# A hybrid attention backbone: the last head and the output tiles of layer 1 become pieces of the listed order

## Chip, cores and metric

The kernel runs on one core of a Trainium2 chip. A core has five engines that run side by side, each through its own queue in order: PE (matrix products), DVE (vectors), ACT (activations), POOL (general vectors) and SP (which here only issues DMAs). The metric is the device time of one execution in microseconds (us); the result is the median over several runs.

## What is computed

Two layers over 1024 latent tokens of width 1024 with 256 context tokens. Layer 0 is multi-head latent attention, layer 1 differential attention, which the change touches:

```python
def combine(o1, o2, gate):
    o = o1 - lam_full.astype(o1.dtype) * o2
    o = rms_norm(o, g_sub) * (1.0 - lambda_init)
    return gated(o, gate)
...
o1, o1_c = prefix_attention(q[:, :, :, 0:1], k[:, :, :, 0], v, ...)
o2, o2_c = prefix_attention(q[:, :, :, 1:2], k[:, :, :, 1], v, ...)
...
x = layer_norm(DEEPNORM_ALPHA * x + gate[:, None, :] * (o @ out_w[i]), ln_g[i], ln_b[i])
```

Eight heads each have two softmaxes over 1280 keys; the second, times lambda, is taken from the first; the result times the values is normed per head and gated with SiLU; then come the output projection, the residual and a layer norm. Only the 1024 latent rows of layer 1 are wanted.

## The kernel before

Everything is float32 in effect: an operand is split into a high and a low part, and a product is three matmuls (`mm3`, L202 to L206), high by high, high by low, low by high.

Layer 1 works in tiles of 128 query rows, 8 tiles (t = 0 to 7) for each of 8 heads (h = 0 to 7). Attention of one tile (`attend`, L1896 on) has these steps, with the names used below: **scores** (five chunks on PE), **maxima** and a bound (DVE), **exponentials** (ACT), sums and the **join** of the two softmaxes (DVE), the **far half** (a split on ACT and DVE and a transposing DMA on SP, tiles `dd` to `pd`), **turns** of the near half (transposes on PE into the PSUM bank `ps_t`, high part `ph` on ACT, low part `pl` on DVE), **values** (30 matmuls on PE into `ps_t`), the output with a square for the norm (ACT), the norm (POOL), and a store of the tile's result to DRAM (`o_d`, SP).

Beside the attention of head h run the projections of head h + 1: keys, queries and values (`ps_s` on PE), with splits, rotary terms and gates on the other engines. Their gate goes through SiLU into `gg` and then to DRAM as `sg_d`.

The order of this work is not written out by hand. `heads1` (from L1664) describes every step as a piece with an engine, a cost, its inputs and outputs, and a due time; `Plan.run` (L1596 on) simulates the five engines and lists the pieces in the order in which it starts them. The due time is the place in the loop plus an offset per kind (table `OFF`, L46); `EPS1` and `AHEAD` say how far a piece may be taken ahead. All five engines then run in exactly that order (`MAN2`). Tiles have rings of buffers: one bank `ps_t`, four `ps_p` and one `ps_c` for scores, two `ps_s`.

Before, that list holds heads 0 to 6 and the projections of head 7. After it stands another stage, written by hand (`step1`, L2083, and the loops behind it), in which only PE's order is fixed and the eight banks go round as one ring `ps_b`:

- `out_open` (L1451) opens buffers in the place of the projections' inputs, and splits four of the eight output weights; their raw form, `z` and `res`, was loaded and multiplied by the layer's gate (`x.gate`, L1891) at the end of the list.
- attention of head 7 (`scores1`, `turn1`, `turn_far`, `values1`, L1356 to L1432), tile by tile.
- beside it, two tiles behind, the output: `out_load` (L1470) fetches the seven finished heads `o_d` and the gates `sg_d` and multiplies them on POOL; `out_turn` (L1480) transposes the tile on PE and splits it into `wx` and `wy`; `out_tile1` (L1501) does 16 groups of three products, adds the residual and takes the layer norm on DVE, ACT and POOL.

Of the kernel before, what the change touches and what calls it, by code (L numbers as in the profile page):

```python
# [9 lines left out]
F32 = mybir.dt.float32  # L10
# [7 lines left out]
P = 128  # L18
# [25 lines left out]
EPS1 = dict(P=0.05, A=0.05, D=0.2, G=0)  # L44
AHEAD = 3.0
SP0, SP1, SP2 = 0.0, 0.3, 3.3  # L46
OFF = {"bound0": -4.5, "bound1": -0.65, "exp0": -0.45, "exp1": -0.65, "far.hi": -4.3, "far.lo": -2.35, "far.move":
       0.25, "g.add": 0.55, "g.bias": -0.5, "g.keep": 0.45, "g.load": 0.4, "g.sum": -0.9, "g.zero": -1.35, "join":
       -0.6, "k.ctx": -5.4, "k.hi": -0.4, "k.lo": -3.7, "k.move": 2.65, "max.c": -0.05, "max0": -5.7, "max1": 0.2,
       "o.hi": 2.55, "o.lo": 0.15, "o.load": -1.65, "o.mul": -1.85, "open": 2.2, "prod": 0.3, "pv": -5.35,  # L50
       "pv.norm": -0.8, "pv.out": -0.05, "pv.sq": -3.0, "pv.store": -2.0, "pv.us": 0.35, "q.hi": -0.6, "q.lo": -0.1,
       "q.move": 1.95, "r.add": 0.45, "r.cos": 1.1, "r.out": 1.4, "r.sin": -1.3, "r.swap": -0.15, "score0": 0.45,
       "score1": 0.4, "scorec": 0.05, "sums": -3.55, "turn.hi0": -1.25, "turn.hi4": -1.2, "turn.lo0": 0.9,
       "turn.lo4": -3.25, "turn0": -0.6, "turn4": 0.5, "v.gate": 1.3, "v.hi": 1.3, "v.keep": 0.7, "v.lo": 1.65,
       "v.octx": -0.25, "v.out": 2.05, "v.pctx": 0.05, "v.silu": 1.2, "v.store": 6.05, "v.turn": -2.25, "w.hi": 1.2,
       "w.lo": 0.4, "w.load": -0.6, "w.root": -1.2, "w.scale": 0.55, "w.sq": 0.95, "w.sum": -6.25, "w.unit": 0.95,
       "w.us": -1.3, "x.gate": 1.15, "x.load": 5.2, "x.mul": 4.6}
# [5 lines left out]
SLOTO = 0, 7000, 7000, 7000, 7000  # L63
# [9 lines left out]
def hybrid_kernel(  # L73
# [1282 lines left out]
    def scores1(h, t):  # L1356

        ks = kt1[h]
        q1, qs = qt1[h]
        ts = slice(t * P, (t + 1) * P)  # L1360
        mx, sm = w1("mx"), w1("sm")
        p = [w1("p0"), w1("p1")]

        def st_of(out, m, c0, n):
            pe.matmul(out, qs[m][:, ts], ks[m][:, c0:c0 + n], start=True, stop=False)
            pe.matmul(out, q1[m][:, ts], ks[m][:, c0:c0 + n], start=False, stop=True)

        st = {}

        def chunk(c0, ms):  # L1370
# [78 lines left out]
    def out_open():  # L1449
# [10 lines left out]
        for k, w in enumerate(pre):  # L1460
# [5 lines left out]
            if k == 0:  # L1466
                out_load(1)
# [737 lines left out]
```

## Time and profile before

| | before |
|---|---|
| median of 3 runs | 1737.77 us (1737.37 to 1739.45) |
| the profiled execution | 1738.9 us, span 1737.1 us |
| PE busy | 1632.8 us (94%) |
| DVE busy | 1252.4 us (72%) |
| ACT busy | 1150.4 us (66%) |
| POOL busy | 903.6 us (52%) |

The span is from the first to the last record of the trace; the execution's own time has a little around it. The listed stage of layer 1 runs from about 950 to 1565 us of the span, the stage written by hand from there to the end. Busy time is what an engine's instructions took; matmuls are pipelined, so their durations overlap and a busy PE need not be at its peak. The granted clock is the share of full speed that PE had. A wait is given with the engine and tile that ended it, the sum, the number and the longest.

### The profile page before, as it was taken

How to read it: one execution, taken by the hardware profiler on the slowest of the kernel's cores; microseconds unless marked ns; L12 is line 12 of the kernel's file. 1: busy time of each engine (PE TensorE's matmuls, PEld its weight loads, DVE VectorE, ACT ScalarE, POOL GpSimd, SP SyncE). 2: the span in 40 equal slices, each digit the busy share in tenths (PEclk: the TensorE clock that was granted, in tenths of full speed). 3: DMA queues.
4: the chain of work that ended last, by engine and by line, in shares of the span. 5: the costliest groups of instructions: out<-in, count | busy, mean ns of one | idle time of the engine just before them, and what ended most of it. 6: DMA issues, size and time to landing. Idle time of an engine off the chain costs nothing.

```text
span 1737.1 us, 36492 instructions
## 1 busy us (share of the span) xinstructions
PE 1632.8 (94%) x14308; PEld 1203.3 (69%) x14308; DVE 1252.4 (72%) x2005; ACT 1150.4 (66%) x2228; POOL 903.6 (52%) x772
## 2 busy tenths in 40 slices
PE   7999999999999999899999999999999999995997
PEld 6989966566656656567776676767676767583776
DVE  7658765566565575746763889898989898976664
ACT  2552167777867867855563887878787878776452
POOL 1522047666867867764645526262626363636454
PEclk9999999999999999999999999999999999997999
DMA  8258530111111121335532344434333344334442
GB/s 311 85 148 245 163 96 23 37 35 39 37 35 39 37 60 26 110 138 185 162 130 69 77 103 96 102 97 103 93 76 96 79 92 107 62 96 137 122 126 79
DMA packets 183930, 171.63 MB, mean 99 GB/s; under 512 B 82023, under 2 KB 159431, under 8 KB 183758
## 3 DMA queue, kind: packets, MB, share of 16 engines
q1 hardware_dynamic: 175358, 161.69, 34.0%
q10 hardware_dynamic: 8400, 7.61, 1.3%
q8 instruction: 112, 1.84, 0.5%
q14 instruction: 60, 0.49, 0.1%
HBM read 98.65 MB, written 27.07 MB: 72 GB/s over the span
## 4 chain that ended last, share of the span: by engine, by line
PE 52%; DVE 26%; ACT 10%; issue 5%; DMA 4%; POOL 3%; POOLq 0%; ACTq 0%; SPq 0%; DVEq 0%
PE ps_a L852 3%; DVE p L1947 3%; DVE mx L1927 3%; PE ps_s L204 3%; PE ps_s L205 3%; PE ps_s L206 3%; PE ps_a L853 3%; PE ps_a L854 3%; PE ps_a L204 3%; PE ps_a L206 3%; PE ps_a L205 3%; PE ps_a L776 2%; ACT p L796 2%; PE ps_b L206 2%; PE ps_b L204 2%
## 5 line engine op out<-in xcount | busy, mean ns | idle before, releaser
L798 POOL TENSOR_TENSOR pl<-p,ph 128x1024 f16<-128x1024 f32 (+1 forms) x176 | 364.5, 2077 | 149.8 <-ACT ph L797 124.0
L796 ACT ACTIVATE p<-ps_a,esc 128x1024 f32<-128x1024 f32 (+1 forms) x176 | 189.0, 1074 | 96.2 <-PE ps_a L854 90.2
L778 DVE TENSOR_REDUCE mx<-ps_a 128x1 f32<-128x1024 f32 x128 | 155.3, 1222 | 130.7 <-PE ps_a L776 130.6
L797 ACT CAST ph<-p 128x1024 f16<-128x1024 f32 (+1 forms) x176 | 177.1, 1006 | 5.5
L1934 ACT ACTIVATE p<-ps_p,mx 128x512 f32<-128x512 f32 x224 | 153.4, 690 | 26.8 <-DVE mx L1929 26.6
L867 PE MATMUL ps_d<-Vh,pl 128*128 128x65 f16 x1344 | 146.6, 195 | 4.5 <-POOL pl L798 4.4
L864 PE MATMUL ps_d<-Vh,ph 128*128 128x65 f16 x1344 | 148.8, 195 | 0.0
L866 PE MATMUL ps_d<-Vl,ph 128*128 128x64 f16 x1344 | 147.6, 193 | 0.0
L1927 DVE TENSOR_REDUCE mx<-ps_p 128x1 f32<-128x512 f32 x224 | 143.8, 680 | 0.1
L864 PEld LDWEIGHTS <-ph 128*128 128x128 f16 x1344 | 123.6, 98 | 18.1 <-issue 4.9
L866 PEld LDWEIGHTS <-ph 128*128 128x128 f16 x1344 | 124.3, 99 | 12.3 <-issue 0.3
L852 PE MATMUL ps_a<-qH,KH 100*128 100x512 f16 x320 | 122.5, 383 | 7.9 <-ACT p L796 3.6
L867 PEld LDWEIGHTS <-pl 128*128 128x128 f16 x1344 | 123.5, 98 | 5.8 <-POOL pl L798 5.8
L853 PE MATMUL ps_a<-qH,KL 96*128 96x512 f16 x320 | 122.2, 382 | 0.0
L854 PE MATMUL ps_a<-qL,KH 96*128 96x512 f16 x320 | 121.5, 380 | 0.0
L1947 DVE SCALAR_TENSOR_TENSOR p<-p,sm,p 128x1280 f32<-128x1280 f32 x56 | 103.5, 1848 | 1.2
L1973 DVE SCALAR_TENSOR_TENSOR pl<-ps_t,lcf,ph 128x512 f16<-128x512 f32 x110 | 67.1, 610 | 28.8 <-ACT ph L1971 28.5
L1906 PE MATMUL ps_p<-KS,Q 128*128 128x512 f16 x224 | 85.0, 379 | 0.0
L1905 PE MATMUL ps_p<-KS,QS 128*128 128x512 f16 x224 | 85.0, 379 | 0.0
L776 PE MATMUL ps_a<-KH,qH 96*128 96x512 f16 x256 | 76.5, 381 | 7.3 <-DVE stkL L201 2.7
L1971 ACT ACTIVATE ph<-ps_t,lcf 128x512 f16<-128x512 f32 x110 | 64.3, 585 | 10.0 <-PE ps_t L1966 9.5
L1988 PE MATMUL ps_t<-vh,ph 128*128 128x128 f16 x330 | 58.1, 219 | 10.5 <-DVE pl L1973 10.5
(540 smaller groups left out, 5606.5 us busy)
## 6 DMA issues: line engine op xcount, KB each, us to landing
ws<-in_dw SPq DMA_DIRECT2D x28, 512.0 KB, 4.7
adw<-in_ada_w SPq DMA_DIRECT2D x24, 512.0 KB, 4.5
adaw<-in_ada_w SPq DMA_DIRECT2D x16, 512.0 KB, 6.4
g<-sg_d SPq DMA_DIRECT2D x16, 512.0 KB, 3.7
sg_d<-gg ACTq DMA_DIRECT2D x40, 128.0 KB, 3.4
o_d<-op SPq DMA_DIRECT2D x7, 640.0 KB, 4.5
xt<-in_xT SPq DMA_DIRECT2D x16, 256.0 KB, 4.0
wgs<-in_w_in SPq DMA_DIRECT2D x32, 128.0 KB, 3.0
```

What stands on the lines that cost most here:

```text
L778: dve.tensor_reduce(mx[:, t, 0:1], ps, axis=AX.X, op=ALU.max)
L796: act.activation(p32[:, :n], st, AF.Exp, scale=esc0)
L797: act.copy(ph[:, :n], p32[:, :n])
L798: pool.tensor_tensor(pl[:, :n], p32[:, :n], ph[:, :n], op=ALU.subtract)
L852: pe.matmul(s_, kh[:nr, ks], QH[:nr, :], start=True, stop=False)
L853: pe.matmul(s_, kl[:DQ, ks], QH[:DQ, :], start=False, stop=False)
L854: pe.matmul(s_, kh[:DQ, ks], QLo[:DQ, :], start=False, stop=True)
L864: pe.matmul(pv[:, t, :], ph[:, ts], Vh[:, k, h, :], start=(k == kcs[0] and t == 0), stop=False, skip_group_check=True)
L866: pe.matmul(pv[:, t, :V0], ph[:, ts], Vl[:, k, h, :], start=False, stop=False, skip_group_check=True)
L867: pe.matmul(pv[:, t, :], pl[:, ts], Vh[:, k, h, :], start=False, stop=(k == NT - 1), skip_group_check=True)
L1927: add(f"max{m}", "D", 0.68, lambda i=i, b_=b_: dve.tensor_reduce(mx.tile[:, 2 + 2 * m + i:3 + 2 * m + i], b_.tile, axis=AX.X, op=ALU.max, ...
L1947: add("join", "D", 1.65, lambda: dve.scalar_tensor_tensor(p[0].tile, p[1].tile, sm.tile[:, 4:5], p[0].tile, op0=ALU.mult, op1=ALU.add), r= ...
```

## The change

The stage written by hand is gone. Head 7's attention is now described by the same `attend` as the others, and the openings, splits of weights, gatings, turns, products and norms of the output tiles are pieces of the same list; so all five engines' order is fixed to the end, and `ps_b` is gone: the output's turns use the one bank `ps_t`, its products the two `ps_s`. Placeholder buffers without data (`PRV`, `H1T`, `OPEN`, `SGT` and others) tell the planner what must be over before a buffer is used again or read back from DRAM. The whole table `OFF` is new, also for the kinds that were there; `AHEAD` goes from 3.0 to 3.75, and `EPS1` of POOL from 0 to 0.2.

```diff
-EPS1 = dict(P=0.05, A=0.05, D=0.2, G=0)
-AHEAD = 3.0
+EPS1 = dict(P=0.05, A=0.05, D=0.2, G=0.2)
+AHEAD = 3.75
...
-       0.25, "g.add": 0.55, "g.bias": -0.5, "g.keep": 0.45, "g.load": 0.4, "g.sum": -0.9, "g.zero": -1.35, "join":
+       3.05, "g.add": 0.6, "g.bias": 2.4, "g.keep": -1.25, "g.load": 0.25, "g.sum": -0.9, "g.zero": 0.35, "join":
...
+ZLAG = 0.5
...
+        def opened():
+            prv.close()
+            place["g"] = a1.enter_context(spool("a1outg"))
...
+        def out_split(k, w, a):
+            H, L = lambda: oHL[k][0], lambda: oHL[k][1]
+            if (k - NOW) % 2:
+                add("x.hi", "A", 1.04, lambda: act.copy(H(), w.tile), r=[OPEN, w], w=[(OHT[k], 0)], hold=0.95, at=a)
+                add("x.lo", "G", 2.85, ...)
+            else:
+                add("x.hi", "A", 1.15, ...)
+                add("x.low", "D", 1.5, ...)
...
+        def out_load(t, a):
+            add("z.o", "S", 4.5, lambda: sp.dma_start(o.tile[:, :DH], o_d[1][ts, :DH]), r=[ODT[t]], w=[OT], new=[o], hold=0.06, at=a)
+            add("z.g", "S", 4.0, lambda: sp.dma_start(gt.tile, sg_d[1][ts, :]), r=[SGT, OPEN], w=[GT], new=[gt], hold=0.06, at=a)
+            add("z.mul", "G", 2.1, ...)
...
+        def out_tile(t, a):
+            for k0, n, ca, cd in ((0, 4, 0.58, 0.69), (4, 3, 0.49, 0.55), (7, 1, 0.27, 0.28)):
+                b = new1("t")
...
+            for hh in range(2):
+                y = new1("s")
+                for k in range(KT):
+                    add(f"z.mm{hh}", "P", 0.7, ...)
+                add("z.add", "D", 0.69, ...)
+                add("z.bn", "D", 0.68, ...)
...
+        add("late", "X", 0.0, opened, w=[PRV, H1T, OPEN], at=g)
+        for i, w in enumerate(raws):
+            out_split(NOW + i, w, g + 0.2 * i)
+        for t in range(NT8):
+            out_load(t, g + t - 1.6 if t > 1 else g + 0.1)
+            nxt = attend(H1 - 1, t, g + t, nxt)
+            if t:
+                out_tile(t - 1, g + t - 1 + ZLAG)
+        attend(None, None, g + NT8, nxt)
+        out_tile(NT8 - 1, g + NT8 - 1 + ZLAG)
         order = pl_.run(EPS1, AHEAD)
...
-        h = H1 - 1
-        out_open()
-        for t in range(SEQ // P):
-            if t >= 2:
-                out_load(t)
-            G = weave(out_tile1(t - 2), out_turns(t - 1), (9, 12)) if t >= 2 else iter(())
-            if t == 2:
-                G = chain(out_turns(0), G)
-            credit[0] = 0
-            step1((h, t), G, SLOTO)
-            for _ in G:
-                pass
```

Where the orders differ at the seam between the list and the last head:

POOL before, from the split of head 7's values (`vl`) on. `z` and `res` are raw output weights, `gate` the layer's gate, `ws` a tile of the seven finished heads, `g` its gates, `sm` and `ss` sums of the softmax and of the norm.

```order
L1856 TENSOR_TENSOR vl_21914<-Vf_21389,vh_21912 128x1280
L1891 TENSOR_TENSOR z_21916<-z_21916,gate_12518 128x1024
L1891 TENSOR_TENSOR res_21919<-res_21919,gate_12518 128x1024
L1891 TENSOR_TENSOR z_21921<-z_21921,gate_12518 128x1024
L1891 TENSOR_TENSOR res_21926<-res_21926,gate_12518 128x1024
L196 TENSOR_TENSOR o_3359_21945<-res_21919,o_3358_21944 128x1024
L196 TENSOR_TENSOR o_3359_21945<-res_21926,o_3358_21944 128x1024
L1475 TENSOR_TENSOR ws_21946<-ws_21946,g_21947 128x896
L1475 TENSOR_TENSOR ws_21953<-ws_21953,g_21954 128x896
L1422 TENSOR_TENSOR sm_21965<-sm_21965,us_20762 128x1
```

POOL of the change, from the last norm of an earlier tile to the second split of weights:

```order
L1759 TENSOR_SCALAR o_3335_21916<-o_3335_21916,ss_21923 128x128
L1670 TENSOR_TENSOR vl_21974<-Vf_21400,vh_21962 128x1280
L1705 TENSOR_TENSOR res_21618<-res_21618,gate_12518 128x1024
L182 TENSOR_SCALAR ss_22026<-ss_22026 128x1
L183 TENSOR_TENSOR ss_22026<-ss_22026,neghalf 128x1
L1759 TENSOR_SCALAR o_3355_22017<-o_3355_22017,ss_22026 128x128
L1746 TENSOR_TENSOR sm_21920<-sm_21920,us_20739 128x1
L1705 TENSOR_TENSOR res_21714<-res_21714,gate_12518 128x1024
L1871 TENSOR_TENSOR ws_21314<-ws_21314,g_22066 128x896
L1860 TENSOR_TENSOR o_3368_22063<-res_21618,o_3367_22062 128x1024
L1871 TENSOR_TENSOR ws_21364<-ws_21364,g_22093 128x896
L1860 TENSOR_TENSOR o_3368_22063<-res_21714,o_3367_22062 128x1024
```

Two multiplications by the gate that stood behind the split of values are now ahead of these rows (`z`), the two others (`res`) and the gatings of tiles 0 and 1 alternate with the splits of weights, and a norm of head 6 stands between them.

ACT before, from the cast of head 7's values on: `ph` is a turn's high part, `o` a split of an output weight, `res` a scaling of one, `p` an exponential of head 7 (first tile `sm_21965`, second `sm_22022`).

```order
L1855 CAST vh_21912<-Vf_21389 128x1280
L200 ACTIVATE ph_21998<-ps_b_22000,lcf 128x512
L200 ACTIVATE ph_21998<-ps_b_22007,lcf 128x256
L1464 ACTIVATE o_3358_21944<-z_21916,gsub 128x1024
L1890 ACTIVATE res_21919<-res_21919,gsub 128x1024
L1388 ACT_TABLE_LOAD
L1388 ACTIVATE p_3367_21967,sm_21965<-ps_b_21986,mx_21964 128x512
L1890 ACTIVATE res_21926<-res_21926,gsub 128x1024
L195 CAST o_3358_21944<-res_21919 128x1024
L1464 ACTIVATE o_3358_21944<-z_21921,gsub 128x1024
L195 CAST o_3358_21944<-res_21926 128x1024
L1388 ACTIVATE p_3367_21967,sm_21965<-ps_b_21990,mx_21964 128x512
```

ACT of the change, in the middle of the same stretch; `sm_22021` is tile 1 of head 7, whose first exponentials stand ahead of these rows, as do all six of tile 0 and the load of their table:

```order
L1724 ACTIVATE ph_22047<-ps_t_22037,lcf 128x512
L1805 ACTIVATE p_3364_22049,sm_22021<-ps_p_21947,mx_21980 128x512
L1704 ACTIVATE res_21714<-res_21714,gsub 128x1024
L1862 ACTIVATE o_3367_22062<-z_21560,gsub 128x1024
L1724 ACTIVATE ph_22047<-ps_t_22068,lcf 128x256
L1805 ACTIVATE p_3364_22049,sm_22021<-ps_p_21954,mx_21980 128x512
L1805 ACTIVATE p_3364_22049,sm_22021<-ps_c_21964,mx_21980 128x256
L1859 CAST o_3367_22062<-res_21618 128x1024
L1862 ACTIVATE o_3367_22062<-z_21667,gsub 128x1024
L1859 CAST o_3367_22062<-res_21714 128x1024
L1823 ACTIVATE dd_22130<-p_3356_22020,lcf 128x512
L1747 ACTIVATE o_3378_22134<-ps_t_22096,sm_21920 128x128
```

The exponentials of two tiles stand ahead of the last three splits of weights, where before one exponential of tile 0 stood ahead of them, behind a split.

SP before, from the loads of raw weights to the gates of the first two output tiles (`sg_d` is written from `gg` and read back as `g`):

```order
L1888 DMA z_21916<-in_out_w 128x1024
L1888 DMA res_21919<-in_out_w 128x1024
L1888 DMA z_21921<-in_out_w 128x1024
L1888 DMA res_21926<-in_out_w 128x1024
L1859 DMA sg_d_98<-gg_21382 128x8x128
L1474 DMA g_21947<-sg_d_98 128x1024
L1474 DMA g_21954<-sg_d_98 128x1024
```

SP of the change, from the last of the four loads of raw weights to the gates:

```order
L1702 DMA res_21714<-in_out_w 128x1024
L1826 DMA_TRANSPOSE pd_21801<-dd_21761 128x8x128
L1762 DMA o_d_100<-o_3313_21754 128x128
L1826 DMA_TRANSPOSE pd_21925<-dd_21912 128x8x128
L1762 DMA o_d_100<-o_3335_21916 128x128
L1826 DMA_TRANSPOSE pd_22024<-dd_21978 128x8x128
L1673 DMA sg_d_98<-gg_21373 128x8x128
L989 DMA wsq_22064<-in_ln_g 128x1024
L1870 DMA g_22066<-sg_d_98 128x1024
L1762 DMA o_d_100<-o_3355_22017 128x128
L1870 DMA g_22093<-sg_d_98 128x1024
L1826 DMA_TRANSPOSE pd_22153<-dd_22130 128x8x128
```

All four loads of weights are over three transposes (`pd`) ahead of the store of the gates, where they stood right before it; that store now comes behind the transpose of tile 0 of head 7; behind the first load of gates stand a store, the second load and a transpose.

406 lines of the change are left out of this document (133 added, 273 removed), and 3 rows, old and new, of the table OFF.

## The prediction

> **What bounds the kernel now.** I read the time in stretches first, then who waits for whom on the tensor engine (PE), then single stretches in order of time. The page's row of the granted clock shows one dent near the end, in the fourth slice from the last:
>
> ```profile
> PEclk9999999999999999999999999999999999997999
> 1414.00:1490.00 76.00, 73.52 (x638) 53.82 (x637) 68.61 (x124) 62.86 (x160) 35.41 (x44) 1.00 0.35 86
> 1560.00:1600.00 40.00, 20.26 (x133) 12.84 (x131) 24.08 (x36) 23.98 (x48) 26.28 (x17) 0.70 0.44 135
> 1600.00:1650.00 50.00, 48.62 (x281) 36.83 (x280) 34.64 (x66) 25.09 (x68) 19.28 (x22) 1.00 0.44 116
> 1650.00:1700.00 50.00, 49.11 (x302) 37.35 (x300) 32.30 (x66) 24.50 (x66) 26.82 (x28) 1.00 0.42 132
> ```
>
> Columns: the stretch, its length, busy time of PE, its weight loads, DVE, ACT, POOL; then clock, DMA share, GB/s. PE is busy for 97% of a stretch inside the list of heads and for 98% once the output tiles run. Only the 40 us where the list ends and the last head begins are poor: 20.26 us busy, at a clock of 0.70. The waits of PE in those 40 us:
>
> ```profile
> PE ps_b L1365 <- ACT p L1388: 11.3, 2, 5.7
> PE ps_b L1401 <- DVE p L1394: 5.1, 1, 5.1
> PE ps_b L1365 <- ACT ps_t L1995: 2.1, 1, 2.1
> PE ps_b L1365 <- DVE pl L201: 1.2, 1, 1.2
> ```
>
> They add up to 19.7 us. The largest is scores (L1365) that want a bank whose exponentials (L1388) stand in ACT's queue behind the splits of the output weights, and those wait for POOL:
>
> ```profile
> 1565.33 2.62 POOL L1856 TENSOR_TENSOR vl<-Vf,vh 128x1280 f16<-128x1280 f32 x1
> 1581.11 5.64 POOL L196 TENSOR_TENSOR o<-res,o 128x1024 fp32r<-128x1024 f32 x2
> 1586.70 4.11 POOL L1475 TENSOR_TENSOR ws<-ws,g 128x896 f32<-128x896 f32 x2
> ```
>
> From 1565.33 POOL does the last split of values, four multiplications of weights by the gate, two splits and two gatings, to 1590.8, in the program's order. The landmarks on PE:
>
> ```profile
> 1559.16 0.27 PE L206 MATMUL ps_s<-wy,h1L 128*128 128x256 f16 x1
> 1559.27 0.22 PE L1988 MATMUL ps_t<-vh,ph 128*128 128x128 f16 x1
> 1560.94 0.27 PE L1365 MATMUL ps_b<-KS,QS 128*128 128x256 f16 x1
> 1601.04 0.50 PE L204 MATMUL ps_b<-oH,wx 128*128 128x512 f32 x1 [0.64 <-ACT wx L195]
> ```
>
> The last projection of the last head is at 1559.16, the first output product at 1601.04: **41.9 us**. In them PE has only attention to do: three tiles of values (30 products each, 1559.27 to 1560.94, so 1.67 us warm) and their scores and turns, some 14 us of work.
>
> **The change part by part.** Both programs hold the same number of instructions of each kind on each engine; only order, PSUM banks and so waits differ. Up to the last projection both do the same work on PE, and after it as well. So the sum has four terms: the transition, the output tiles, the tail, the earlier heads.
>
> **Transition.** In the new order the exponentials of tiles 0 and 1 of the last head stand ahead of the weights' splits on ACT, two gate multiplications stand on POOL before the last split of values, and the weights are loaded 20 to 30 us earlier (order of ACT, POOL and SP above). The loads' cost is nothing while they ride behind the moves of queries; all four are requested before the transition. What ends last then is ACT's own queue. Its pitches:
>
> ```profile
> 1553.15 0.69 ACT L1971 ACTIVATE ph<-ps_t,lcf 128x512 f16<-128x512 f32 x1
> 1553.91 0.69 ACT L1934 ACTIVATE p<-ps_p,mx 128x512 f32<-128x512 f32 x1
> 1554.59 0.68 ACT L1934 ACTIVATE p<-ps_p,mx 128x512 f32<-128x512 f32 x1
> 1555.26 0.47 ACT L1934 ACTIVATE p<-ps_c,mx 128x256 f32<-128x256 f32 x1
> 1559.86 1.28 ACT L1858 ACT_TABLE_LOAD   x1
> 1561.15 1.15 ACT L1858 ACTIVATE gg<-gg,uw 128x1024 f32<-128x1024 f32 x1
> 1562.21 0.70 ACT L1952 ACTIVATE dd<-p,lcf 128x512 f16<-128x512 f32 x1
> 1562.82 0.35 ACT L1994 ACTIVATE o<-ps_t,sm 128x128 f32<-128x128 f32 x1
> 1563.20 0.28 ACT L1995 ACTIVATE ps_t<-o 128x128 f32<-128x128 f32 x1
> 1563.99 1.26 ACT L1855 CAST vh<-Vf 128x1280 f16<-128x1280 f32 x1
> 1576.06 1.14 ACT L1890 ACTIVATE res<-res,gsub 128x1024 f32<-128x1024 f32 x1
> 1577.10 1.03 ACT L195 CAST o<-res 128x1024 fp32r<-128x1024 f32 x1
> ```
>
> Between the last projection and the first turned output tile the new order gives ACT 9 wide exponentials (0.67 from start to start: 6.0), 4 narrow (0.45: 1.8), 4 turns' high parts (0.6 and 0.4: 2.0), two table loads (2.6), the SiLU (1.1), three far halves (0.62: 1.9), three outputs with squares (0.38 and 0.3: 2.0), the cast of values (1.3), two copies of the last projection (0.8), two scalings and four splits of weights (1.03: 6.2), one split of a turned tile (0.6): **26.3 us**. Waits that this order does not fill: after a tile's last exponential DVE needs its sums and the join (0.65 and the 1.55 of the row below), a low part of a turn (0.4), PE the values (1.67), with four hand-overs 4.8 us, before ACT can take the output; for tile 0 ACT has 3.3 us of other work there (the cast, a turn, a scaling, a far half), for tile 1 3.7 us (three splits, a far half): waits of 1.5 and 1.1 us, and 0.5 for the maxima of tile 2. From the turned tile's high part to the first product come DVE's low part, one more turn and the hand-overs, 1.6 us. Sum **31.0 us**. Against 41.9: 10.9 earlier. PE has by then done two more pieces of scores than before (4 products of 0.216: 0.9).
>
> ```profile
> 1559.52 1.55 DVE L1947 SCALAR_TENSOR_TENSOR p<-p,sm,p 128x1280 f32<-128x1280 f32 x1
> 1563.65 0.59 PE L1365 MATMUL ps_b<-KS,QS 128*128 128x512 f16 x1 [2.10 <-ACT ps_t L1995]
> 1563.50:1564.50 1.00, 0.85 (x3) 0.29 (x3) 0.80 (x2) 0.97 (x3) 0.73 (x2) 0.52 0.00 0
> 1567.50:1568.50 1.00, 0.75 (x7) 0.43 (x5) 0.60 (x2) 0.87 (x2) 0.45 (x1) 1.00 0.84 319
> ```
>
> After a gap of 2.10 us the clock stood at 0.52 and was 1.00 again about 3.5 us later. My count leaves PE gaps of 2.3 to 2.8 us in the new transition too, so I charge 1.3 us for products that run at half clock on the path. Term: -10.9 - 0.9 + 1.3 = **-10.5 us**; ends: -14 (ACT without waits, clock full) and -6 (each of PE's three bursts of values at half clock on the path, and one join more waited for).
>
> The Trainium skill, "TensorE: Matmul & The Clock Gate", Part 1, says that the clock halves only after an idle window of about 3.4 us. Here 2.10 us sufficed, so the row decides. By the page the new gaps would not cool PE, and the term would be -11.8.
>
> Two waits come on SP, which works in order. The loads of gates (L1870) wait for the store of the last head's gates, and that now stands behind a transpose (L1826) that waits for the join of tile 0; behind the load stand the last store of head 6, the second load and the next transpose, which tile 1's values want.
>
> ```profile
> 1567.57 0.59 SPq L1859 DMA_DIRECT2D sg_d<-gg  x1
> 1575.57 0.80 SPq L1474 DMA_DIRECT2D g<-sg_d  x2
> DMA to landing us min/median/max: 3.4/3.9/4.2
> DMA to landing us min/median/max: 3.7/3.7/3.7
> ```
>
> The last two lines are the landing of such a store (L1859) and such a load (L1474); the store of before waited behind 2 MB of weights. From the join of tile 0, some 16 us after the last projection: 1.2 (transpose) + 3.9 + 3.7 + 2.1 (gating) + 2 (turn, split, hand-overs) = 29 us. That is 2 us under ACT's 31.0: hidden, and the first thing to be late if ACT is faster.
>
> **Output tiles.** From the first output product PE has 127 us of work, before as after. Before, idle was 2.3 us per 100 (1600 to 1700); the list's own stretch above has 3.3%. Six users a tile (two turns, values, three output turns) now share the one bank ps_t where eight banks went round; no row shows that. Least: no loss, -1.5 if the idle of before goes as well. Most: the two waits on this bank in the heads,
>
> ```profile
> PE ps_t L1988 <- DVE pl L1973: 10.5, 13, 1.1
> PE ps_t L1966 <- ACT ps_t L1995: 5.1, 4, 1.6
> ```
>
> 15.6 us over 55 tiles, 0.28 a tile for three hand-overs, twice that for six: 4.5 us in 8 tiles, and 8.8 if one hand-over in each tile costs the 1.1 of the longest. I take the list's rate, 1% of 127: **+1.3 us**, since products of 0.25 us stand between all hand-overs.
>
> **Tail.**
>
> ```profile
> 1727.99 1.37 DVE L1522 TENSOR_TENSOR z<-ps_b,res 128x512 f32<-128x512 f32 x2 [2.19 <-PE ps_b L206]
> 1729.28 1.27 DVE L1523 BATCH_NORM_STATS2 bs<-z 128x6 f32<-128x512 f32 x2
> ```
>
> Before, both halves of the last tile are added and summed after PE is done. Now the first half ends two groups of products earlier, 1.5 us, and its 1.3 us on DVE goes beside PE; before it was one group. **-0.5 us**; ends 0 and -1.
>
> **Earlier heads.** The whole table of offsets is new, so seven heads are reordered as well. PE's work between the turns and the values of a tile, by the two orders, is a median of 2.2 us in both; I take **0**. Its ends: half of the 15.6 us of waits just shown gone (-8), or a third more of them (+5).
>
> Sum: -10.5 + 1.3 - 0.5 + 0 = -9.7. The profiled execution took 1738.9 us (span 1737.1), so 1729.2, and the median of the runs shown, 1737.8, is 1.1 below it: **1728.1 us**.
>
> **The rivals.** (1) *The bank decides, slower than before.* If ps_t's hand-overs are not covered, PE stands in each of 8 tiles. The gain of 11.0 us is gone at 1.4 us a tile; at 2.2 us a tile the time is 1737.8 - 11.0 + 17.6 = 1744. For: values follow the second turn after one group and two scores, 0.75 + 0.86 us, and ACT's 0.4, DVE's 0.4 and three hand-overs come near that. Against: DVE has room there (66.9 of 100 us busy from 1600 to 1700). Chance 0.09. (2) *The transition is not shortened.* The chain over SP and POOL ends last instead: if the store of gates or a split of weights on POOL comes 10 us later than I count, the first product stays at 41 us: 1738. For: 4.11 and 5.64 us of POOL remain. Against: two of the four multiplications are out of the way. Chance 0.11. (3) *The heads gain too.* Idle in the list falls from 3.3% to the 2.3% of the output tiles, over 600 us: 6 to 8 us more, 1721. For: PE waits there are all hand-overs of one bank. Against: equal distances. Chance 0.15. (4) *PE stays warm*, as the page's window would have it, and the 1.3 us are not paid: 1727. For: gaps shorter than that window. Against: the 2.10 us gap. Chance 0.10.
>
> **How the numbers follow.** A measurement of this kernel tells 0.2% (3.5 us) from no change: faster is below 1734.3, slower above 1741.2. Forecast 0.55, the rivals 0.09, 0.11, 0.15, 0.10. Faster: 0.55 + 0.15 + 0.10 = 0.80; same 0.11; slower 0.09. Range: down to the middle of rival 3 with a warm clock, 1717, up to rival 2 with some loss, 1739; beyond lie rival 1 and the outer part of rival 3.
>
> **What would show it.** Right: in the new trace, last projection to first output product about 31 us, PE's waits there in pieces below 3 us, the clock's dent shallower; output tiles every 17.2 to 17.8 us; matmul end to span end about 8 us. Wrong: PE waiting on ps_t for over 1 us a tile (rival 1); the first product waiting for the gating of the tile (rival 2); a shorter time from 960 to the last projection (rival 3).

## The result, and the profile after

| | before | after |
|---|---|---|
| median | 1738.4 us (1737.4 to 1739.5, 4 runs) | 1714.7 us (1710.3 to 1717.8, 4 runs) |
| ratio | | 0.9862, 95% interval 0.9835 to 0.9889 |
| the profiled execution, its span | 1738.9, 1737.1 us | 1710.3, 1708.5 us |
| PE busy | 1632.8 us (94%) | 1621.1 us (95%) |

The change saves 23.7 us; the forecast was 9.7, and 1714.7 us lies below the forecast's range of 1717 to 1739. The row of the granted clock on the page of after, to be held against that of before:

```profile
PEclk9999999999999999999999999999999999998999
```

The dent is still there and shallower. Stretches of after, with the columns of before's:

```profile
1414.00:1490.00 76.00, 73.89 (x653) 55.52 (x652) 68.90 (x128) 62.02 (x160) 37.30 (x46) 1.00 0.33 77
1545.00:1590.00 45.00, 32.36 (x201) 23.35 (x199) 34.30 (x52) 31.60 (x70) 25.81 (x19) 0.85 0.46 119
1590.00:1640.00 50.00, 50.00 (x332) 39.62 (x330) 35.04 (x64) 22.01 (x54) 28.83 (x27) 1.00 0.45 132
1640.00:1690.00 50.00, 50.00 (x319) 39.05 (x317) 39.93 (x70) 25.84 (x66) 28.11 (x26) 1.00 0.36 111
```

Once the output tiles run, PE is busy for 50.00 of 50 us: PE never waits there for the one bank ps_t with its six users. The waits of PE in after's transition, from 1544 to 1578 us:

```profile
PE ps_p L1776 <- ACT p L1805: 9.6, 6, 2.7
PE ps_t L1741 <- DVE pl L1726: 2.0, 2, 1.5
PE ps_t L1884 <- ACT ps_t L1748: 1.0, 1, 1.0
```

19.7 us of waits have become 12.6, in pieces of 2.7 at most, three quarters of them for exponentials in ACT's queue. The landmarks on PE's timeline of after (first and seventh turn of values, last projection, first output product, last product):

```profile
1015.33 0.38 PE L1641 MATMUL ps_s<-idr,rr 128*128 128x128 f32 x2
...
1529.71 0.38 PE L1641 MATMUL ps_s<-idr,rr 128*128 128x128 f32 x2
...
1544.03 0.27 PE L210 MATMUL ps_s<-wy,h1L 128*128 128x256 f16 x1
...
1577.05 0.77 PE L208 MATMUL ps_s<-oH,wx 128*128 128x512 f32 x1
...
1700.06 0.39 PE L210 MATMUL ps_s<-o,wy 128*128 128x512 f32 x1
```

and the two turns of before:

```profile
1018.13 0.38 PE L1827 MATMUL ps_s<-idr,rr 128*128 128x128 f32 x2
...
1545.83 0.38 PE L1827 MATMUL ps_s<-idr,rr 128*128 128x128 f32 x2
```

A turn of values (L1827, now L1641) comes once a head, so from the first to the seventh lie six heads of the list. The two profiles differ by 28.6 us:

| stretch | before | after | difference |
|---|---|---|---|
| span's start to the first turn of values | 1018.1 | 1015.3 | -2.8 |
| six heads | 527.7 | 514.4 | **-13.3** |
| seventh turn to last projection | 13.3 | 14.3 | +1.0 |
| last projection to first output product | 41.9 | 33.0 | **-8.9** |
| output tiles, to the last product | 127.2 | 123.0 | **-4.2** |
| tail | 8.9 | 8.4 | -0.4 |

The first row is mostly layer 0, where both programs are the same; in the other profiles below it lies between 1015 and 1022, so it is the spread of executions. The profiled execution of after is also its fastest. Nine products of projections run inside the six heads in before and behind the seventh turn in after, so 1.0 us only moves between the second row and the third. What is left to explain are the six heads, for which I had taken nothing.

### The profile page after: what moved, and what is told of

It is laid out like the page before. It is cut to its first block, busy times and chain, and to the rows that moved or that the text cites. A ratio compares the mean times of both kernels' runs of the same rounds, so it can differ in the third digit from the quotient of the medians.

```text
span 1708.5 us, 36480 instructions
## 1 busy us (share of the span) xinstructions
PE 1621.1 (95%) x14308; PEld 1204.9 (71%) x14308; DVE 1249.1 (73%) x2005; ACT 1150.5 (67%) x2228; POOL 905.0 (53%) x772
## 4 chain that ended last, share of the span: by engine, by line
PE 55%; DVE 21%; ACT 13%; issue 4%; DMA 3%; POOL 3%; SPq 0%; POOLq 0%; ACTq 0%; DVEq 0%
PE ps_s L208 4%; PE ps_s L210 4%; PE ps_s L209 4%; ACT p L1805 4%; PE ps_a L856 3%; PE ps_a L857 3%; PE ps_a L858 3%; PE ps_a L208 3%; PE ps_a L210 3%; PE ps_a L209 3%; DVE mx L1798 3%; DVE p L1818 2%; PE ps_a L780 2%; ACT p L800 2%; PE ps_d L871 2%
## 5 line engine op out<-in xcount | busy, mean ns | idle before, releaser
L1805 ACT ACTIVATE p<-ps_p,mx 128x512 f32<-128x512 f32 x256 | 175.7, 690 | 31.2 <-DVE mx L1800 30.5
L1798 DVE TENSOR_REDUCE mx<-ps_p 128x1 f32<-128x512 f32 x256 | 164.3, 681 | 1.9 <-PE ps_p L1777 1.9
L1726 DVE SCALAR_TENSOR_TENSOR pl<-ps_t,lcf,ph 128x512 f16<-128x512 f32 (+1 forms) x128 | 78.3, 611 | 42.8 <-ACT ph L1724 42.1
L1776 PE MATMUL ps_p<-KS,QS 128*128 128x512 f16 x256 | 97.9, 382 | 9.6 <-ACT p L1805 9.6
L1724 ACT ACTIVATE ph<-ps_t,lcf 128x512 f16<-128x512 f32 (+1 forms) x128 | 74.9, 585 | 39.2 <-PE ps_t L1719 38.2
L1777 PE MATMUL ps_p<-KS,Q 128*128 128x512 f16 x256 | 98.2, 384 | 0.0
L182 POOL TENSOR_SCALAR ss<-ss 128x1 f32<-128x1 f32 x64 | 18.8, 294 | 118.9 <-ACT ps_t L1748 117.2
```

Source lines behind the costliest of these rows:

```text
L1798: add(f"max{m}", "D", 0.68, lambda i=i, b_=b_: dve.tensor_reduce(mx.tile[:, 2 + 2 * m + i:3 + 2 * m + i], b_.tile, axis=AX.X, op=ALU.max, ...
L1805: add(f"exp{m}", "A", 0.78 if n == 512 else 0.57, lambda i=i, c0=c0, n=n, b=b, lo=lo: act.activation(p[m].tile[:, c0:c0 + n], b.tile[:, lo ...
```

## Where six heads lose 13 us

The six heads of before, then of after, with the columns of the stretches above:

```profile
1018.13:1545.83 527.70, 511.48 (x4370) 369.71 (x4369) 478.62 (x852) 424.18 (x1085) 256.56 (x309) 1.00 0.40 95
1015.33:1529.71 514.38, 504.94 (x4360) 370.73 (x4359) 464.02 (x850) 421.48 (x1081) 249.39 (x309) 1.00 0.40 94
```

Half of the 13.3 us are waits: PE is not busy for 16.2 us in before and for 9.4 in after. The largest waits that are left in after:

```profile
PE ps_t L1741 <- DVE pl L1726: 3.9, 5, 1.0
PE ps_t L1719 <- ACT ps_t L1748: 3.5, 3, 1.2
```

The other half, 6.5 us, is counted as busy time of PE: 1.0 us are the nine products, and the rest are longer distances, most of them behind the last product of a group. What caused these was not tested. DVE, for nearly the same instructions, is busy for 14.6 us less.

In before PE's largest waits recur at fixed places of each head. One is at the fourth tile behind the turn of values, here in the second head of the list, on PE's timeline:

```profile
1145.90 0.22 PE L1988 MATMUL ps_t<-vh,ph 128*128 128x128 f16 x1 [1.07 <-DVE pl L1973]
```

Values wait for the second low part of the turns. DVE's timeline of before, in the 14 us ahead of it:

```profile
1131.78 3.09 DVE L1947 SCALAR_TENSOR_TENSOR p<-p,sm,p 128x1280 f32<-128x1280 f32 x1
...
1140.93 1.28 DVE L1730 SCALAR_TENSOR_TENSOR wx<-ws,uw,wx 128x1024 f16<-128x1024 f32 x1
1142.13 2.29 DVE L1730 SCALAR_TENSOR_TENSOR wy<-ws,uw,wy 128x1024 f16<-128x1024 f32 x1
...
1145.37 0.47 DVE L1973 SCALAR_TENSOR_TENSOR pl<-ps_t,lcf,ph 128x256 f16<-128x256 f32 x1
```

and POOL's:

```profile
1130.88 2.64 POOL L1856 TENSOR_TENSOR vl<-Vf,vh 128x1280 f16<-128x1280 f32 x1
...
1141.16 2.18 POOL L1755 TENSOR_TENSOR kr<-kr,rsw 128x512 f32<-128x512 f32 x1 [1.52 <-DVE kr L1753]
```

The join took 3.09 us where the prediction had quoted 1.55, and a split of weights 2.29 beside one of 1.28. Both times a POOL operation was running: the join began at 1131.78, POOL's split of values ended at 1133.52, and 1133.52 + 1.35 is the join's end. DVE **stood until POOL was done**, and the profile counts that as busy time of DVE, not as a wait (e5, e7 and e8 below test this reading). DVE has no gap here, so what it stands reaches the low part and PE. The groups of the join in before and after, over the six heads:

```profile
L1947 DVE SCALAR_TENSOR_TENSOR p<-p,sm,p 128x1280 f32<-128x1280 f32 x48 | 91.1, 1898 | 1.0
```

```profile
L1818 DVE SCALAR_TENSOR_TENSOR p<-p,sm,p 128x1280 f32<-128x1280 f32 x48 | 81.3, 1693 | 1.2
```

The same 48 joins take 1.90 us in the mean before and 1.69 after. In after the join of that tile starts ahead of POOL's split:

```profile
1126.05 1.55 DVE L1818 SCALAR_TENSOR_TENSOR p<-p,sm,p 128x1280 f32<-128x1280 f32 x1
```

```profile
1126.93 3.15 POOL L1670 TENSOR_TENSOR vl<-Vf,vh 128x1280 f16<-128x1280 f32 x1 [1.17 <-ACT vh L1669]
```

So the theory, called "held" below: the new table puts DVE's operations with two inputs in SBUF beside fewer POOL operations, and that is the 13 us. It is a theory at this point, and e11 and e13 show that it is not the whole of it. The first question was whether the table, without the new stage, carries them at all.

## Experiments

All runs, with the medians, the ratio to runs of before on the same chip, and two stretches of the one execution that was profiled:

| run | us | ratio, 95% interval | six heads | seventh turn to first output product |
|---|---|---|---|---|
| before | 1738.4 | | 527.7 | 55.2 |
| after | 1714.7 | 0.9835 to 0.9889 | 514.4 | 47.3 |
| e1 new table, old stage | 1725.0 | 0.9905 to 0.9933 | 514.2 | 55.6 |
| e2 old table, new stage | 1764.3 | 1.0119 to 1.0156 | 530.4 | 78.5 |
| e3 one offset, old stage | 1740.5 | 0.9989 to 1.0013 | 530.4 | 54.5 |
| e4 low part, old stage | 1739.3 | 0.9985 to 1.0009 | 528.1 | 55.0 |
| e5 join first, old stage | 1734.1 | 0.9957 to 0.9985 | 525.4 | 54.4 |
| e6 gate later, new stage | 1714.3 | 0.9839 to 0.9874 | 514.4 | 49.1 |
| e7 copy first, new stage | 1708.7 | 0.9811 to 0.9845 | 510.4 | 47.5 |
| e8 cosine first, new stage | 1705.1 | 0.9788 to 0.9821 | 507.2 | 48.0 |
| e9 narrow gate, new stage | 1710.1 | 0.9811 to 0.9851 | 514.2 | 47.9 |
| e10 three, new stage | 1705.7 | 0.9787 to 0.9826 | 508.1 | 47.3 |
| e11 three, old stage | 1733.5 | 0.9955 to 0.9981 | 524.4 | 54.9 |
| e12 PE new | 1746.3 | 1.0023 to 1.0052 | 534.6 | 55.9 |
| e13 the rest new | 1733.9 | 0.9958 to 0.9980 | 522.1 | 56.4 |
| e14 ACT and DVE new | 1753.8 | 1.0075 to 1.0107 | 539.7 | 58.1 |
| e15 all but POOL new | 1737.5 | 0.9986 to 1.0011 | 525.0 | 59.4 |

**e1 and e2: the table and the stage, one at a time.** e1 is the kernel before with the new numbers:

```diff
-EPS1 = dict(P=0.05, A=0.05, D=0.2, G=0)
-AHEAD = 3.0
+EPS1 = dict(P=0.05, A=0.05, D=0.2, G=0.2)
+AHEAD = 3.75
-OFF = {"bound0": -4.5, "bound1": -0.65, ...
+OFF = {"bound0": -5.35, "bound1": -0.75, ...
```

> The kernel before with the new offsets (all but one, turn4, without which the order of heads 0 to 6 is that of the changed kernel on every engine), AHEAD 3.75 and EPS1 of POOL 0.2; the last stage stays the one written by hand. Theory 'the order of the heads' (the new table takes 2.2 us out of each head, whatever stands behind the list): six heads take 514 us from the first turn of values to the seventh in place of 528, last projection to first output product stays near 42 us, time 1738.4 - 12 = 1726, 1723 to 1729. Rival 'one list' (the gain in the heads belongs to the longer list or is only the difference of two executions): 1736 to 1740, six heads near 528.

e2 is the changed kernel with the old numbers, the same lines the other way round, while the kinds of the last stage keep theirs.

> The changed kernel with the old offsets for all kinds that had one, AHEAD 3.0 and EPS1 of POOL 0: the order of heads 0 to 6 is that of before on every engine, the last head and the output are pieces of the list. Theory 'the order of the heads': six heads near 528 us again; of the gain stay the transition (8.9), the output tiles (4.2) and the tail (0.4): 1738.4 - 13.5 = 1725, 1721 to 1729. Rival 'one list': 1712 to 1717, as the changed kernel. If the new offsets are also what makes the transition and the output tiles short: above 1730.

e1 came as the theory of the heads' order said: 514.2 us for six heads, 1725.0 us, 14.3 below before (1739.3 on its chip). (Its last projection falls 4 us later behind the seventh turn, so from there to the first output product it takes 38.4 us and not 42; the last column has the whole.) The table alone is worth more than half of the change. From e1 to after, which is the new stage with the table held fixed, it is 10.3 us more, close to the forecast's 9.7. That is partly luck: between the profiles of e1 and after, the stretch to the first output product loses 8.3 us, the output tiles 4.3 and the tail 0.4, where the forecast had -10.5, +1.3 and -0.5. e2 confirms the heads (530.4) but not the sum: the new stage with the old numbers is 25 us **slower** than before. From its last projection to its first output product, 63 us pass. SP's queue in that stretch:

```profile
1582.58 1.24 SPq L1826 DMA_TRANSPOSE pd<-dd  x1
1583.92 0.52 SPq L1762 DMA_DIRECT2D o_d<-o  x1
1592.45 11.82 SPq L1826 DMA_TRANSPOSE pd<-dd  x2
1604.33 0.57 SPq L1673 DMA_DIRECT2D sg_d<-gg  x1
1604.94 0.63 SPq L989 DMA_DIRECT2D wsq<-in_ln_g  x1
1608.05 0.80 SPq L1870 DMA_DIRECT2D g<-sg_d  x2
```

The store of the last head's gates (L1673) stands behind two more transposes than in after and comes at 1604, 43 us after the last projection at 1561.0; in after it comes at 1563.3, 19 us behind. The late store is what rival 2 of the prediction feared, but it does not explain the 63 us by itself: POOL's first gating waits 1.2 us for the gates and starts at 1613.2, and the last pieces of the chain to the first output product, at 1624.0, are DVE's (a split of 2.6 us, a join of 3.3). And in e2's output tiles PE waits three times for the bank, the wait that rival 1 named:

```profile
PE ps_t L1884 <- DVE pl L1726: 6.2, 3, 2.6
```

Both kinds of wait occur with the old table and neither in after, so what the new stage is worth depends on the table too.

**e3, e4: one place in the old order.** e3 changed one offset (q.move from 1.95 to -5.7). The planner's order came out as before on every engine, so the premise of its expectation was wrong; it is a second run of before. It shows that six heads spread between 527.7 and 530.4 us. The 1.7 us of products in its expectation and in the next one belong to the third tile; at the fourth, before has 4.1 us of products between turn and values, and PE waits there all the same.

> The kernel before with one offset changed, q.move from 1.95 to -5.7: SP's order stays, PE gets 3.2 us of products in place of 1.7 between the second turn and the values of the fourth tile behind the turn of values, in each of heads 1 to 6; a few instructions of ACT and DVE trade places. Theory 'one place a head': the wait of 1.23 us for pl there is gone in six heads, -7.4: 1731, 1728 to 1734. Rival 'the wait only goes elsewhere' (DVE or ACT is late at the next hand-over instead): 1736 to 1740.

e4 moves one instruction of DVE a head:

```diff
+        for t in [t for t in order if t["kind"] == "turn.lo4"]:
...
+            if len(w) == 2 and ...:
+                order.insert(w[1], order.pop(i))
```

> The kernel before with one instruction of DVE moved in each of six heads: the second low part of the turns of that fourth tile goes ahead of the second split of weights and the sums, some 2.5 us earlier; PE, ACT, POOL and SP keep their order. Theory 'DVE's queue at one place': values no longer wait for pl there (1.23 us a head), -7.4: 1731, 1728 to 1734. Rival 'PE's distance': 1.7 us of products between turn and values are too short whatever DVE does, over 0.6 us of the wait stays and the time is 1735 to 1739.

Neither: the wait for pl at that tile went, and nothing was gained (528.1 us). PE's next wait of e4 in the same head:

```profile
1147.69 0.66 PE L1966 MATMUL ps_t<-idr,p 128*128 128x128 f32 x4 [1.12 <-ACT ps_t L1995]
```

The next turn now stands 1.12 us for the bank, until ACT's square behind the values has been done. One hand-over had hidden the next.

**e5: the join free.** Two exchanges a head in the old order, so that the join starts before POOL's split of values:

```diff
 act: ..., exp,
+     r.out,
      v.hi, turn.hi4,
-     r.out,
      w.hi, ...
 dve: ..., sums,
-     turn.lo4, join,
+     join, turn.lo4,
      max.c, ...
```

> The kernel before with two exchanges in each of six heads, at the third tile behind the turn of values: on DVE the join goes ahead of the second low part, on ACT one copy of keys (r.out) ahead of the cast of values (v.hi), so that POOL's split of values (v.lo) starts after the join has started. PE, POOL and SP keep their order. In the trace of before this join lasts 3.09 us in each of six heads while v.lo runs, 1.55 elsewhere. Theory 'held' (DVE operations with two inputs in SBUF stand while POOL works, and DVE is full in this stretch): the join lasts 1.55, six heads take 518 to 520 us in place of 528 to 530, time 1739.3 - 9 = 1730, 1728 to 1733. Rival 'the wait goes elsewhere', as with the moved low part: 1737 to 1741.

Between the two. The joins of the six heads:

```profile
L1947 DVE SCALAR_TENSOR_TENSOR p<-p,sm,p 128x1280 f32<-128x1280 f32 x48 | 86.0, 1792 | 1.2
```

5.1 us less than in before, and the time is 4.8 us lower (0.9957 to 0.9985), half of what I expected. Held joins cost time, but new waits come up at the third and sixth tiles.

**e6 and e9: the transition.** In after, DVE's and POOL's timelines show a held operation there too:

```profile
1559.02 2.92 DVE L1824 SCALAR_TENSOR_TENSOR dd<-p,lcf,dd 128x512 f16<-128x512 f32 x1
```

```profile
1559.05 2.35 POOL L1705 TENSOR_TENSOR res<-res,gate 128x1024 f32<-128x1024 f32 x1
```

The transpose and the store of gates wait for that dd. e6 moves the multiplication (`x.gate`) behind the next norm and `pv.us`. e9 narrows two such multiplications to 8 of 1024 columns: that kernel leaves out the gate in the other columns of two of the eight output weights.

```diff
+        later(g_[v_ + 1], g_[v_ + 3], ("z", "res"))
```

> The changed kernel with one instruction of POOL moved in the transition: the first multiplication of a raw weight by the gate behind the split of values goes behind the norm that followed it; all other engines keep their order. Theory 'held': the far half's low part (dd), 2.92 us while that multiplication runs, takes 0.75; the transpose on SP, the store of gates and their load, and ACT's exponentials behind the next maxima come 1.5 to 2.2 us earlier; last projection to first output product 33.0 - 1.8 = 31.2 us (30.6 to 31.8), time 1714.7 - 1.8 = 1713. Rival 'ACT's own queue' (26.3 us of work in order set the end whatever DVE does): 32.7 to 33.4 us. Third case, the weight is late for its split on ACT: above 33.4.

```diff
-            add("x.gate", ..., pool.tensor_tensor(w.tile, w.tile, gate1, op=ALU.mult), ...
+            gn = 8 if k % 2 else D
+            add("x.gate", ..., pool.tensor_tensor(w.tile[:, :gn], w.tile[:, :gn], gate1[:, :gn], op=ALU.mult), ...
```

> The changed kernel with the two multiplications by the gate on POOL that fall between the last split of values and the first gating narrowed to 8 of 1024 columns: two of the eight output weights are used without their gate in the other columns. The order on every engine is unchanged. Theory 'held': the far half's low part takes 0.75 us in place of 2.92 and the low part of an output weight 1.4 in place of 2.37; with the clock of the changed kernel's transition (0.81 in the mean) last projection to first output product 33.0 - 2.0 = 31.0 us (30.3 to 31.8); with the clock of the run with the later gate (0.63) up to 33. Rival 'ACT's own queue': 32.7 to 33.4 us at the clock of the changed kernel. Time 1712 to 1715.

Both freed that dd (0.74 and 0.77 us), and neither shortened the transition: 34.8 and 33.6 us from last projection to first product. In e6 the clock was lower (0.72), and the values of tile 1 ran at half speed; PE's timeline of e6:

```profile
1557.76 0.27 PE L1741 MATMUL ps_t<-vh,ph 128*128 128x128 f16 x1 [2.11 <-DVE pl L1726]
1557.82 0.31 PE L1742 MATMUL ps_t<-vl,ph 128*128 128x128 f16 x1
1557.93 0.31 PE L1743 MATMUL ps_t<-vh,pl 128*128 128x128 f16 x1
```

Their starts are 0.107 us apart; in after 0.056, behind a gap of 1.53 us. In e9 the whole transition had a clock of 0.85, as after has (0.82), so the clock does not explain it; there the next dd was held in its turn, and the low part of a weight, on DVE's timeline of e9:

```profile
1577.78 2.78 DVE L1825 SCALAR_TENSOR_TENSOR dd<-p,lcf,dd 128x512 f16<-128x512 f32 x1
...
1582.46 3.45 DVE L1864 SCALAR_TENSOR_TENSOR o<-z,gsub,o 128x1024 fp32r<-128x1024 f32 x1
```

So what DVE's standing costs the transition stays open: each time it moved on to a later operation. Nor do the medians tell these two runs from after: the intervals overlap.

**e7 and e8: the same theory on the new order.** e7 puts the copy of values ahead of an output weight's high part on ACT, so that POOL's low part no longer starts 0.14 us ahead of a join:

```diff
 act: ..., exp,
+     v.out,
      o.hi,
-     v.out,
      pv.out, ...
```

> The changed kernel with one exchange on ACT in each of three heads (those that split an output weight): the copy of values out of PSUM (v.out) goes ahead of the high part of the output weight (o.hi), so that the low part on POOL (o.lo), 0.14 us ahead of a join until now, starts behind it. Theory 'held': that join takes 1.55 us in place of 3.56 in three heads, PE's wait of 1.35 us for the turn behind it is gone there: six heads 514.4 - 4 = 510.4 us, time 1714.7 - 4 = 1711. Rival 'the wait goes elsewhere': six heads 513.5 to 515, time 1713 to 1717.

The join of that tile in after, then in e7:

```profile
1267.35 3.56 DVE L1818 SCALAR_TENSOR_TENSOR p<-p,sm,p 128x1280 f32<-128x1280 f32 x1
```

```profile
1269.14 1.55 DVE L1818 SCALAR_TENSOR_TENSOR p<-p,sm,p 128x1280 f32<-128x1280 f32 x1
```

Six heads take 510.4 us, the expected number. The medians alone do not tell e7 from after, since the intervals overlap. e8 puts a product of two tiles in SBUF (`r.cos`) directly behind the shuffle at 14 places, ahead of POOL's product of the shuffled tile:

```diff
 dve: ..., r.swap,
+     r.cos,
      turn.lo0,
-     r.cos,
      ...
```

> The changed kernel with one exchange on DVE at 14 places, two a head: the cosine product of the queries (r.cos, two inputs in SBUF) goes ahead of the low part that stood between it and the shuffle, so that it starts before POOL's sine product and not in the middle of it. Theory 'held': it takes 0.68 us in place of 1.36; the wait of 1.0 us for pl at the seventh tile, in four of six heads, shrinks by about 0.7: six heads 514.4 - 2.8 = 511.6 us, time 1712. Rival 'POOL is held in its place': the sine product starts or ends 0.6 us later, the sum of rotary terms too, and six heads stay at 514 to 515, time 1713 to 1717.

More than expected: 507.2 us, 1705.1 us, 9.6 below after. Its group in after, then in e8:

```profile
L1567 DVE TENSOR_TENSOR rr<-rr,cosB 128x512 f32<-128x512 f32 x12 | 16.3, 1359 | 0.0
```

```profile
L1567 DVE TENSOR_TENSOR rr<-rr,cosB 128x512 f32<-128x512 f32 x12 | 8.3, 692 | 0.4
```

1.36 us became 0.69. What I had not counted, and what no run separates from the rest: DVE's later operations now also met POOL at other moments, and the joins that e7 had freed were free here without that exchange (1566 ns in the mean, down from 1693). PE's waits in these six heads of e8, where after has 3.9, 3.5 and 1.3 us in its three largest groups:

```profile
PE ps_t L1719 <- DVE pl L1726: 1.2, 4, 0.3
PE ps_t L1719 <- DVE p L1818: 0.7, 2, 0.5
```

e10 joins e7 and e8 and adds a third exchange, of which nothing was left to gain:

> The changed kernel with the exchanges of the two runs before (copy of values ahead of the output weight's high part on ACT, cosine product ahead of the low part on DVE) and a third on DVE in five heads, the first split of weights (w.lo, 2.2 us there, held by POOL's sum of rotary terms) ahead of the low part that it waited behind. Theory 'held': the copy brings nothing more, since that join was already free in the run with the cosine first; the split takes 1.3 us, and the waits left at the fourth and fifth tile (3.0 us over six heads) shrink: six heads 507.2 - 2 = 505, time 1705.1 - 2 = 1703, 1701 to 1705. Rival 'nothing waits there any more for DVE': 1704 to 1706.5, six heads 507.

1705.7 us and 508.1 us: the same as e8. Both are faster than before and after.

**e11: the exchanges in the old order.** e5 and, once a head, that of e8:

> The kernel before with the two exchanges of 'join first' (join ahead of the second low part, copy of keys ahead of the cast of values, in six heads) and, once a head, the cosine product ahead of the low part on DVE. Theory 'held': the cosine product takes 0.7 in place of 1.4 us at the sixth tile, the low part behind it and PE's wait for it at the seventh tile (4.4 us over six heads) shrink, and the 2.8 us of waits that had come up at the sixth tile go: six heads 525.4 - 5 = 520 us, time 1734.1 - 5 = 1729, 1727 to 1731; then four exchanges in the order of before give over half of what the new table gives. Rival: what was held comes back at another place, 1732 to 1736.

The rival: 524.4 us, 1733.5 us, hardly more than e5. The theory "held" falls as the whole explanation of the 13 us. DVE's busy time in these six heads is 467.4 us: of the 14.6 us that the new table saves there e11 saves 11.2, and of the 13.3 us of the heads only 3.3. A reason that works on the new order does little on the old one; that other hand-overs end last there is the likely reading, seen in e4 and e5 and not tested further.

**e12 to e15: whose order is it.** The kernel before, each engine's sequence in the list prescribed, either the old one or that of e1:

```diff
-                        if t["pri"] > low + ahead and t["pri"] > self.step + ahead:
+                        if t["i"] != seq[e][pos[e]]:
```

> The kernel before, with PE's order in heads 0 to 6 taken from the new table (that of the run with the new table and the old stage) and the orders of ACT, DVE, POOL and SP left as they were. Theory 'held' (the gain comes from where DVE's operations stand beside POOL's, set by ACT, DVE, POOL and SP): six heads 525 to 530 us, time 1735 to 1740. Rival 'PE's distances' (3.2 us of products in place of 1.7 between turn and values of the third tile, and the like, are what covers the hand-overs): six heads 516 to 522, time 1726 to 1732.

> The reverse: the kernel before with the orders of ACT, DVE, POOL and SP in heads 0 to 6 from the new table and PE's order left as it was. Theory 'held': six heads 515 to 521 us, time 1726 to 1731. Rival 'PE's distances': 525 to 530, 1735 to 1740. If both this run and the one with PE's order alone stay above 523, it takes both together.

> The kernel before with ACT's and DVE's order in heads 0 to 6 from the new table, and PE, POOL and SP as they were. If the place of the join ahead of POOL's split of values (set by ACT and DVE) and the sum of gates (g.add) moved out of the full stretch are enough: six heads 515 to 521 us, 1726 to 1731. If POOL's own order or SP's loads are part of it: 522 to 528.

> The kernel before with the new order on PE, ACT, DVE and SP in heads 0 to 6 and POOL's order as it was. If POOL's order does nothing of its own: six heads 513 to 516 us, time 1724 to 1728, as the run with the new table and the old stage. If POOL's own order is where the held time was saved: 518 to 526.

| six heads, us | the others old | the others new |
|---|---|---|
| PE's order old | 527.7 to 530.4 | 522.1 |
| PE's order new | 534.6 | 514.2 |

PE's new order **costs** 4 to 7 us with the old order around it and **saves** 8 with the new one. In e13 DVE is busy for 463.5 us, as little as in after, and six heads still take 522.1. In e12 PE's waits for the low part, 9.6 us in before, are the largest of the heads:

```profile
PE ps_t L1990 <- DVE pl L1975: 13.5, 13, 2.9
```

ACT and DVE alone, without POOL and SP, are 10 us slower; without POOL's new order (e15), the rest give 3 to 5 of the 13 us in the heads and nothing in the median; the stretch behind them is 4 us longer in its profile. No engine's order carries the gain by itself, so the third case of e13's expectation (both stay together) is what was found, with a part of 6 us for the others alone.

## Why the prediction was wrong, step by step

- **Earlier heads, 0.** This step failed. I took PE's work between the turns and the values of a tile, found a median of 2.2 us in both orders, and concluded that nothing changes. Six heads changed by -13.3 us, and e1 shows 14.3 us from the table alone. The median hid that at the third tile of five of the six heads the work went from 1.7 to 3.2 us. And the distance was the wrong thing to look at: at the fourth tile of before PE has 4.1 us of products and still waits 1.07 us, because DVE's queue, where a join stood for 3.09 us, ends last. e12 shows that PE's new distances alone save nothing. The waits were in the prediction's own rows (15.6 us of the heads), with -8 as the utmost; they fell by 6.8 us. Freed waits were not all: my sum had no term for PE's busy time, which fell by about as much. Rival 3 had the sign and half of the size, with too small a chance.
- **Transition, -10.5.** Near in size, right in mechanism only in part: three quarters of PE's waits end with ACT's exponentials, with gaps of PE of 2.42, 2.69 and 2.30 us where 2.3 to 2.8 were counted. 31.0 us and 1.3 for the clock make 32.3; it took 33.0. With the 0.9 us of scores done ahead the term measures -9.8. But the chain of work that ended last in these 33.0 us spends 13.0 on ACT and 12.0 on DVE, held far half (2.92) and a split of weights (2.37) included, where my sum had ACT's 26.3 us of work one behind the other. That both come to nearly the same time is partly luck.
- **Output tiles, +1.3.** Wrong in sign. The stretch went by -4.2 us, of which 0.9 are the scores done ahead: -3.3. The bank's loss, taken from the list's rate, was zero in after; e2 shows 6.2 us of it under another order, so the price hangs on the order and not on the bank. Most of the rest is that output products follow each other at 0.246 us in place of 0.253 in the mean (383 of them, 2.7 us), and 1.8 us of that are before's waits, which went.
- **Tail, -0.5.** It measured -0.4: after's last halves on DVE no longer wait for one another.

```profile
1699.13 0.69 DVE L1901 TENSOR_TENSOR z<-ps_s,res 128x512 f32<-128x512 f32 x1 [4.89 <-PE ps_s L210]
1699.85 0.69 DVE L1903 BATCH_NORM_STATS2 bs<-z 128x6 f32<-128x512 f32 x1
1700.49 0.69 DVE L1901 TENSOR_TENSOR z<-ps_s,res 128x512 f32<-128x512 f32 x1
```

- **The clock.** The charge for half clock was in place: 0.85 from 1545 to 1590, with no gap of PE above 2.7 us; what it cost in time was not measured apart. The Trainium skill, "TensorE: Matmul & The Clock Gate", Part 1, would have had PE warm; the rows differ, and they decide.
- **What is not settled:** by what waits the new order saves its 13 us, of which DVE's standing is a part; which pairs of engines save the 8 us that PE's order brings on top of the others; and what DVE's standing costs the transition.

## What to carry to other kernels

A new table of priorities is an edit of everything that it sorts: before the new part is costed, the old part's order has to be compared place by place on all engines, and the run that separates the two (new numbers, old stage) says first which term is in question. An engine that shows no idle time may still be standing: hold the mean of a group against its shortest member, and look at what runs beside the long ones. And where a wait is removed in a chain of hand-overs, ask for the next one: e4 gained nothing, e5 half, and the same kind of exchange gave all of its gain in e7.

## What the runs showed of the hardware

- DVE operations that read two tiles in SBUF stand while POOL runs an operation on two wide tiles, whatever their own size: the join 3.56 us beside POOL's 2.35 us split, 1.55 alone; the far half's low part 2.92, 0.74 alone; a scalar product of one column 0.73, 0.22 alone (L1944). Reductions out of PSUM (0.68) and low parts with one input in PSUM (0.74) kept their times. Not every POOL operation holds them: in the six heads of after, twelve such DVE operations began beside the one-column power of POOL's norm (L183), and none of them was longer. It also goes the other way: when DVE's cosine product started first in e8, POOL's product took 1.77 us in place of 1.27. The records do not tell close starts apart: e8's cosine product starts 0.05 us ahead of POOL's and held it, after's far half 0.03 us ahead and was held.

```profile
1157.50 0.69 DVE L1567 TENSOR_TENSOR rr<-rr,cosB 128x512 f32<-128x512 f32 x1
1157.55 1.77 POOL L1568 TENSOR_TENSOR rsw<-rsw,sinB 128x512 f32<-128x512 f32 x1 [1.77 <-DVE rsw L1566]
```

The Trainium skill, "GPSIMD Engine Reference", Section 8 (Key points), says that GpSimd shares its SBUF interfaces with VectorE and contends with instructions that have two SBUF inputs; the runs agree, for POOL's wide operations.
- PE's clock fell after short gaps, but not after each: in after a gap of 2.42 us was followed by 1.2 us at full speed, and only then by half; a gap of 1.53 us left the values behind it at full speed, one of 2.11 us in e6 did not. In the profiles' records of the clock each stretch at half speed ahead of the last product lasts 3.41 us or a multiple of it (3.41, 6.83 and 3.41 in after's transition), which fits a count of idle time by windows of that length. Over all runs, from 950 to 1700 us, PE's records leave at least 49% of the 3.41 us ahead idle at each of 48 drops from full speed, and at most 55% where the clock stayed.
